# HGRN2 values in two passes over pairs of token tiles, with value-weight buffers of their own

## The chip, the cores and the metric

The kernel runs on one core of one Trainium2 chip. The metric is the device time of one execution in microseconds (us), lower is better. Times are medians of several executions; the trace comes from one further execution that was profiled. In the trace, PE is TensorE (PEld its weight loads), DVE is VectorE, ACT is ScalarE, POOL is GpSimd, SP is SyncE, which here issues the DMAs of the weights.

## The reference, cut to what matters

The reference is one layer of a hybrid decoder trunk on 512 tokens with a model width of 1024, all in float32:

```
h = rmsnorm(x)
z = h @ w_in                       # columns: q, f, i (values), g of HGRN2, then those of MLA and two gates
o_a = hgrn2(q, f, i, g)            # 8 heads, key and value width 128, recurrent state
o_b = mla(...)                     # 8 heads of latent attention
x = x + (sigmoid(ga) * (o_a @ w_branch_hgrn) + sigmoid(gb) * (o_b @ w_branch_mla)) @ w_out
x = x + moe(rmsnorm(x))            # 64 experts in 8 groups, two per token
out = rmsnorm(x)
```

In HGRN2 each head has a query, a decay (f), a value (i) and an output gate (g), each a projection of h with 1024 x 128 weights. The value of head h is `h @ w_in[:, 2048 + 128 h : 2048 + 128 (h + 1)]`, used as it is, with no nonlinearity.

## The kernel before, in words

The 512 tokens are T = 4 tiles of 128; the width of 1024 is KT = 8 tiles of 128. Most projections are made to near float32 precision from two rounded halves: a weight block comes by DMA into a raw buffer, ACT rounds it into a high part (`split`, L90) and another engine, here mostly POOL, takes the difference as the low part (L91). A product is then three matmuls: high by high, high by low, low by high. The normalised input lies transposed in SBUF in the same two parts (`hT`).

**The order of the stages.** Latent projections and rotary parts, latent attention (`mla`), HGRN2 (`hgrn`), the two branch products with their gates (L204 to L230), the output product with the routing (L249 to L273), and the mixture of experts (`moe`), in which the expert weights are streamed from HBM through a ring of buffers. No order is written out by hand around the change: the framework's scheduler gives each engine a fixed order at compile time, in which instructions that come earlier in the program go first where both are ready, and later ones fill the gaps. On the chip each engine works its own order off and waits at an instruction whose inputs are late.

**HGRN2.** For each head, `project` (L678) makes three projections by `proj` (L635): the decay, the query and the gate. Each loads 512 KB of weights with `wtile` (L275), splits them, and runs 24 matmuls of 512 columns into a PSUM tile `z`. The pool of `z` tiles (`zps`, L155) has two buffers. The pool of the weights (`wp`, L157) has two buffers each of `wraw`, `whi` and `wlo`, 4 KB per partition each; a raw buffer is free when POOL has taken the low part, a `whi`/`wlo` pair is free when its matmuls are done. All weight loads go through SP in order. The body of a head (L711 to L806) is a chain of small DVE products (L717, L719, L762, L763, L778, L791 among them), each followed by small matmuls into `lv` and `mx1`, copies by ACT (L771, L773, L784, L789), and at its end the norm of the head's output: squares on ACT (L801), `rsqrt` on DVE (L105, L114), a scaling on ACT (L805). `close` (L666) transposes that output and multiplies it by the gate, one head later.

**The values.** They are made for two heads at a time, 256 columns wide, by `value_weights` and `values`. The first call (L408, L449) is made ahead of the attention, for heads 0 and 1. The others are made in `hgrn` at L704, when h is 1, 3 and 5, ahead of the projections of head h + 1. In the scheduled order their matmuls fill the gaps of the body of head h - 1, so the bodies of heads 0, 2 and 4 have values beside them, and the projections of head h + 1 follow. `value_weights` makes two blocks of 512 rows by 256 columns with `wtile`, so it takes both `whi` and both `wlo` buffers. `values` takes both `z` tiles, of two token tiles each, and runs over the weight tiles outside and over all four token tiles inside, 96 matmuls of 256 columns; then ACT copies both `z` tiles to `vh` (L632).

Of the kernel before, what the change touches and what calls it, by code (L numbers as in the profile page):

```python
# [10 lines left out]
F32 = mybir.dt.float32  # L11
F32R = mybir.dt.float32r
# [8 lines left out]
T = S // 128  # L21
KT = D // 128
# [54 lines left out]
class Trunk:  # L77
# [206 lines left out]
    def latent(self, st, gl, hT, wp):  # L284

        tc, nc, a, ident, sm, gT = self.tc, self.nc, self.a, self.ident, self.sm, self.gT
        w_in = a["w_in"][0]
# [10 lines left out]
        with tc.tile_pool(name="c", bufs=1, reuse_waits="tile") as cp, tc.tile_pool(name="cps", bufs=4, space=PSUM, reuse_waits="tile") as cps:  # L298
# [40 lines left out]
            ps = cps.tile([128, 8], F32, name="tr", bufs=2)  # L339
# [37 lines left out]
            for t in range(T):  # L377
                if t + 1 < T:
                    columns_of(t + 1)
                ps = cps.tile([128, QR], F32, name="c")  # L380
# [10 lines left out]
            for t in range(T):  # L391
                ps = zps.tile([128, CW - QR], F32, name="z") if t < 2 else cps.tile([128, CW - QR], F32, name="c")
                project(ps, wk, t)
                cacc.append(ps)
            ps = cps.tile([128, 38], F32, name="tr", bufs=2)
# [12 lines left out]
            vw = self.value_weights(wp, 0)  # L408
# [37 lines left out]
                        nc.tensor.transpose(tr[:, h], qs[:, i * 4 + h].rearrange("p a c -> p (a c)"), self.identr)  # L446
                    nc.scalar.copy(out=qpT[:, i * 4:i * 4 + 4, t * 128:(t + 1) * 128], in_=tr)

            self.vals = {0: self.values(hT, vw, self.hv)}  # L449


            a0, a1 = gT[:, 8:16], gT[:, 16:24]
# [62 lines left out]
    def mla(self, lat, obT, wp, hT):  # L515
# [6 lines left out]
        with tc.tile_pool(name="att", bufs=2, reuse_waits="tile") as ap, \  # L522
# [19 lines left out]
            def heads(h):  # L542
# [14 lines left out]
                return qT, kT  # L557

            values_of = {0: values(0)}
            qk = heads(0)  # L560
            for h in range(H):
                qT, kT = qk
                if h % 2 == 1 and h + 1 < H:
                    values_of[h + 1] = values(h + 1)
# [42 lines left out]
            e.tensor_tensor(out=u, in0=y, in1=sin, op=OP.mult)  # L607
            e.tensor_tensor(out=o, in0=t, in1=u, op=op)

    def value_weights(self, wp, h):  # L610

        w_in = self.a["w_in"][0]
        return [self.wtile(wp, w_in[kp * 512:(kp + 1) * 512, 2048 + h * 128:2048 + h * 128 + 256], 4, 256,
                           self.nc.gpsimd) for kp in range(KT // 4)]

    def values(self, hT, weights, pool):

        nc = self.nc
        v = pool.tile([128, T, 256], F32, name="vh", bufs=1)
        ps = [self.zps.tile([128, 2, 256], F32, name="z") for _ in range(2)]  # L620
        for kp, (hi, lo) in enumerate(weights):
            for k in range(4):
                kt = kp * 4 + k
                for t in range(T):
                    ts = slice(t * 128, (t + 1) * 128)
                    L, R = [hT[0][:, kt, ts], hT[1][:, kt, ts]], [hi[:, k], lo[:, k]]
                    for n, (l, r) in enumerate(((0, 0), (0, 1), (1, 0))):
                        nc.tensor.matmul(ps[t // 2][:, t % 2], lhsT=L[l], rhs=R[r],
                                         start=(kt == 0 and n == 0 and t % 2 == 0),
                                         stop=(kt == KT - 1 and n == 2), skip_group_check=True)  # L630
        for u in range(2):
            nc.scalar.copy(out=v[:, 2 * u:2 * u + 2], in_=ps[u])  # L632
        return v

    def proj(self, hT, wp, c0):  # L635
# [18 lines left out]
    def hgrn(self, st, hT, oaT, wp):  # L654
        tc, nc, a, ident, sm = self.tc, self.nc, self.a, self.ident, self.sm
        gT, lb, oml = self.gT, self.lb, self.oml
        w_in = a["w_in"][0]
        hg = st.enter_context(tc.tile_pool(name="hg", bufs=1, reuse_waits="tile"))
# [37 lines left out]
        vals = self.vals  # L696
        self.open = None
        now = project(0)
        for h in range(H):
            P, k, qq, g = now  # L700
            q3 = qq[:, :, 0:128]
            vh = vals[h - h % 2]
            if h % 2 == 1 and h + 1 < H:
                vals[h + 1] = self.values(hT, self.value_weights(wp, h + 1), (self.hv, hg)[(h + 1) // 2 % 2])  # L704
            if h + 1 < H:
                now = project(h + 1)
            close()
# [25 lines left out]
            for m, c0 in ((2, 64), (8, 256)):  # L733
                ks = hg.tile([128, S], F32, name="ks", bufs=2)
# [14 lines left out]
                for d, l0, l1 in ((1, 0, 96), (2, 96, 160), (3, 160, 192)):  # L749
                    w = (4 - d) * m  # L750
# [7 lines left out]
            for m in (32, 64):  # L758
                nb = S // (2 * m)
                ks = hg.tile([128, nb, m], F32, name="ks", bufs=2)  # L760
# [5 lines left out]
                for b in range(nb):  # L766
                    r = (b * 2 * m) % 128
                    c = (0 if m == 32 else 128) + (b * 2 * m) // 128 * m
                    self.mm(x1[r:r + m, c:c + m], ks[:, b], qp[:, b], True, True)
            for r in (0, 64):  # L770
                nc.scalar.copy(out=at[r:r + 32, :, r + 32:r + 64],  # L771
                               in_=x1[r:r + 32, 0:128].rearrange("p (t j) -> p t j", t=T))
# [3 lines left out]
            ks = hg.tile([128, T - 1, 128], F32, name="ks", bufs=2)  # L776
# [513 lines left out]
```

## Time and profile before

| what | us |
|---|---|
| median of 3 runs | 1615.59 |
| lowest and highest of them | 1612.76, 1617.44 |
| the profiled execution, its own time | 1614.09 |
| span of the profiled execution, first to last instruction | 1612.3 |
| PE busy in the span | 1389.1 (86%) |
| DVE, ACT, POOL busy | 595.7, 342.7, 268.1 |

The profiled execution lies 1.79 us above its own span and 1.50 us below the median of the runs. A busy share over the whole span mixes stages with different limits, so the rows further down take the stages one by one. In a row of a timeline the columns are start, duration, engine, line, operation, output from input, shape and count, and in brackets the idle time before it with what ended that.

### The profile page before, as it was taken

The numbers are of one execution on the slowest core, as the hardware profiler recorded it, in microseconds if no ns is written. First come the engines' busy times: TensorE is split into PE (matmuls) and PEld (weight loads), VectorE is DVE, ScalarE is ACT, GpSimd is POOL, SyncE is SP. The second block draws the span as 40 slices with busy tenths as digits, with TensorE's granted clock in tenths as the row PEclk, the third lists the DMA queues.
The fourth block names the chain that finished last, engine by engine and source line by source line (L and its number), as shares of the span: only waits on it lengthen the run. The fifth ranks groups of instructions, "written<-read, shape, count | busy, mean of one in ns | idle before, by whom it ended". The sixth has DMA issues, their size and how long they took to land. (4 is left out here: it accounts for less than half of the span.)

```text
span 1612.3 us, 20371 instructions
## 1 busy us (share of the span) xinstructions
PE 1389.1 (86%) x8282; PEld 846.0 (52%) x8282; DVE 595.7 (37%) x1444; ACT 342.7 (21%) x754; POOL 268.1 (17%) x294
## 2 busy tenths in 40 slices
PE   5999999999999999988897798788688788779784
PEld 5878787778788889933333133133233223223322
DVE  7648686676873333531120120120211112012023
ACT  5456523332242322420000000010000000000012
POOL 4321233332100000021110111011011011011012
PEclk9999999999999999998998899898898899899897
DMA  6111232222144337599999999999999999999995
GB/s 185 58 44 34 57 85 66 66 66 66 53 134 136 97 92 270 230 398 430 430 428 429 430 428 428 429 429 430 429 428 429 429 429 428 429 428 428 430 418 189
DMA packets 124767, 456.35 MB, mean 283 GB/s; under 512 B 11854, under 2 KB 93436, under 8 KB 97532
## 3 DMA queue, kind: packets, MB, share of 16 engines
q1 hardware_dynamic: 121852, 454.52, 70.4%
q8 instruction: 67, 1.10, 0.3%
q10 hardware_dynamic: 2816, 0.47, 0.2%
q14 instruction: 32, 0.26, 0.0%
HBM read 452.87 MB, written 2.10 MB: 282 GB/s over the span
## 5 line engine op out<-in xcount | busy, mean ns | idle before, releaser
L82 PE MATMUL h<-ck,xT 128*32 128x512 f32 x2048 | 313.7, 667 | 122.0 <-DMA ck<-in_expert_w 107.4
L82 PEld LDWEIGHTS h<-ck,xT 128*32 128x32 f32 x2048 | 75.2, 121 | 347.2 <-issue 164.6
L1104 POOL TENSOR_SCALAR t<-cst,slb,wts 128x128 f32<-128x128 f32 x64 | 50.4, 791 | 964.4 <-PE ga L1085 709.4
L1165 DVE TENSOR_TENSOR x<-cb,x 128x512 f32<-128x512 f32 x120 | 82.9, 691 | 289.0 <-PE cb L82 289.0
L82 PE MATMUL y<-ck,hid 128*32 128x512 f32 (+2 forms) x1088 | 170.4, 584 | 16.0 <-ACT hid L1144 9.4
L91 POOL TENSOR_TENSOR wlo<-wraw,whi 128x1024 fp32r<-128x1024 f32 (+3 forms) x52 | 97.6, 1877 | 213.4 <-ACT whi L90 185.8
L82 PE MATMUL z<-hTh,whi 128*128 128x512 f32 x320 | 127.7, 399 | 5.4 <-ACT vh L632 5.3
L1085 PEld LDWEIGHTS ga<-t,wo 128*128 128x128 f32 x1024 | 117.1, 192 | 25.5 <-issue 24.1
L82 PE MATMUL z<-hTh,wlo 128*128 128x512 f32 x320 | 126.7, 396 | 0.0
L82 PE MATMUL z<-hTl,whi 128*128 128x512 f32 x320 | 126.2, 394 | 0.0
L1085 PE MATMUL ga<-t,wo 128*128 128x128 f32 x1024 | 123.2, 278 | 1.2 <-DVE t L1082 1.2
L82 PE MATMUL cb<-xT,owT 128*128 128x512 f32 (+2 forms) x256 | 120.9, 604 | 2.4 <-DVE xT L1181 2.2
L90 ACT CAST whi<-wraw 128x1024 fp32r<-128x1024 f32 (+3 forms) x84 | 77.5, 922 | 172.9 <-PE z L82 94.5
L1139 DVE TENSOR_TENSOR t<-h,t 128x512 f32<-128x512 f32 x16 | 11.1, 691 | 258.9 <-PE h L82 258.9
L82 PEld LDWEIGHTS y<-ck,hid 128*32 128x32 f32 x1088 | 43.8, 111 | 110.0 <-issue 92.3
L82 PEld LDWEIGHTS cb<-xT,owT 128*128 128x128 f32 x256 | 40.3, 188 | 83.5 <-DVE x L1165 46.9
L1161 ACT COPY xT<-y 128x512 f32<-128x512 f32 x30 | 17.6, 585 | 257.4 <-PE y L82 257.4
L1144 ACT COPY hid<-ga 128x512 f32<-128x512 f32 x16 | 9.4, 585 | 293.6 <-PE ga L1142 293.6
L82 PEld LDWEIGHTS z<-hTh,whi 128*128 128x128 f32 x320 | 60.7, 190 | 18.2 <-ACT vh L632 5.9
L1138 DVE TENSOR_TENSOR t<-h,t 128x512 f32<-128x512 f32 x16 | 11.1, 691 | 155.6 <-ACT t L1137 155.6
L82 PEld LDWEIGHTS z<-hTh,wlo 128*128 128x128 f32 x320 | 60.4, 189 | 12.4
L82 PEld LDWEIGHTS z<-hTl,whi 128*128 128x128 f32 x320 | 60.6, 189 | 11.7
(352 smaller groups left out, 2185.0 us busy)
## 6 DMA issues: line engine op xcount, KB each, us to landing
ck<-in_expert_w SPq DMA_DIRECT2D x164, 2048.0 KB, 34.0
ck<-in_expert_w SPq DMA_DIRECT2D x52, 1024.0 KB, 15.0
wraw<-in_w_in SPq DMA_DIRECT2D x48, 512.0 KB, 4.0
wraw<-in_w_branch_mla SPq DMA_DIRECT2D x8, 512.0 KB
wraw<-in_w_branch_hgrn SPq DMA_DIRECT2D x8, 512.0 KB, 4.0
wo<-in_w_out SPq DMA_DIRECT2D x8, 512.0 KB, 6.1
xt<-in_x SPq DMA_DIRECT2D x4, 512.0 KB, 7.5
wraw<-in_mla_w_ukv SPq DMA_DIRECT2D x16, 128.0 KB, 2.5
```

The source lines that it names most:

```text
L82: self.nc.tensor.matmul(ps, lhsT=l, rhs=r, start=start, stop=stop)
L90: self.nc.scalar.copy(out=hi, in_=src)
L91: (eng or self.nc.vector).tensor_sub(out=lo, in0=src, in1=hi)
L1085: nc.tensor.matmul(ps[kt // 4][:, kt % 4], lhsT=self.h2[t][:, kt], rhs=oh[:, t], start=(t == 0 and kt % 4 == 0), stop=(t == T - 1), skip_g ...
L1104: nc.gpsimd.tensor_scalar(out=ow[:, t], in0=iota, scalar1=slot(t, 0), scalar2=wts[:, t, 0:1], op0=OP.is_equal, op1=OP.mult)
L1138: nc.vector.tensor_mul(out=sg, in0=rows(h1), in1=sg)
L1139: nc.vector.tensor_mul(out=sg, in0=rows(h3), in1=sg)
L1144: nc.scalar.copy(out=hid, in_=ps)
L1161: nc.scalar.copy(out=ysb[:, hs], in_=y[half])
L1165: nc.vector.tensor_add(out=self.x2[:, t, hs], in0=ps, in1=self.x2[:, t, hs])
```

## The change

The values are computed for token tiles 0 and 1 over all eight weight tiles, copied out, and then for token tiles 2 and 3. Each pass takes one `z` tile. The first call, ahead of the attention, passes `(range(T),)` and stays one pass over all four tiles. For the three calls in `hgrn`, the high and low parts of the value weights get tiles of their own in the pool `hg`, `vwh` and `vwl` of 8 KB per partition each and one buffer each; the raw weights still come through `wraw` and SP, and ACT and POOL still split them in two blocks.

```diff
-            self.vals = {0: self.values(hT, vw, self.hv)}
+            self.vals = {0: self.values(hT, vw, self.hv, (range(T),))}
...
-    def value_weights(self, wp, h):
-
-        w_in = self.a["w_in"][0]
-        return [self.wtile(wp, w_in[kp * 512:(kp + 1) * 512, 2048 + h * 128:2048 + h * 128 + 256], 4, 256,
-                           self.nc.gpsimd) for kp in range(KT // 4)]
-
-    def values(self, hT, weights, pool):
+    def value_weights(self, wp, h, pool=None):
+
+        src = lambda kp: self.a["w_in"][0][kp * 512:(kp + 1) * 512, 2048 + h * 128:2048 + h * 128 + 256]
+        if pool is None:
+            return [self.wtile(wp, src(kp), 4, 256, self.nc.gpsimd) for kp in range(2)]
+        hi, lo = [pool.tile([128, KT, 256], F32R, name=f"vw{i}") for i in "hl"]
+        for kp in range(2):
+            raw = wp.tile([128, 4, 256], F32, name="wraw")
+            self.nc.sync.dma_start(out=raw, in_=src(kp).rearrange("(k p) c -> p k c", p=128))
+            ks = slice(kp * 4, kp * 4 + 4)
+            self.split(raw, hi[:, ks], lo[:, ks], self.nc.gpsimd)
+        return [(hi[:, kp * 4:kp * 4 + 4], lo[:, kp * 4:kp * 4 + 4]) for kp in range(2)]
+
+    def values(self, hT, weights, pool, pairs=((0, 1), (2, 3))):

         nc = self.nc
         v = pool.tile([128, T, 256], F32, name="vh", bufs=1)
-        ps = [self.zps.tile([128, 2, 256], F32, name="z") for _ in range(2)]
-        for kp, (hi, lo) in enumerate(weights):
-            for k in range(4):
-                kt = kp * 4 + k
-                for t in range(T):
+        for ts_ in pairs:
+            ps = [self.zps.tile([128, 2, 256], F32, name="z") for _ in ts_[::2]]
+            for kt in range(KT):
+                hi, lo = [w[:, kt % 4] for w in weights[kt // 4]]
+                for t in ts_:
                     ts = slice(t * 128, (t + 1) * 128)
-                    L, R = [hT[0][:, kt, ts], hT[1][:, kt, ts]], [hi[:, k], lo[:, k]]
-                    for n, (l, r) in enumerate(((0, 0), (0, 1), (1, 0))):
-                        nc.tensor.matmul(ps[t // 2][:, t % 2], lhsT=L[l], rhs=R[r],
+                    for n, (l, r) in enumerate(((0, hi), (0, lo), (1, hi))):
+                        nc.tensor.matmul(ps[t // 2 - ts_[0] // 2][:, t % 2], lhsT=hT[l][:, kt, ts], rhs=r,
                                          start=(kt == 0 and n == 0 and t % 2 == 0),
                                          stop=(kt == KT - 1 and n == 2), skip_group_check=True)
-        for u in range(2):
-            nc.scalar.copy(out=v[:, 2 * u:2 * u + 2], in_=ps[u])
+            for u, z in enumerate(ps, ts_[0] // 2):
+                nc.scalar.copy(out=v[:, 2 * u:2 * u + 2], in_=z)
         return v
...
-                vals[h + 1] = self.values(hT, self.value_weights(wp, h + 1), (self.hv, hg)[(h + 1) // 2 % 2])
+                vals[h + 1] = self.values(hT, self.value_weights(wp, h + 1, hg), (self.hv, hg)[(h + 1) // 2 % 2])
```

## Rows read from the trace of the kernel before

**Rows 1.** Busy time of each engine in four stretches: HGRN2, the branch products, the output product with the routing, and the experts. Columns: stretch, its length, busy time (and count) of PE, PEld, DVE, ACT, POOL, then the granted TensorE clock, the busy share of the DMA engines and GB/s.

```profile
180.00:465.00 285.00, 270.94 (x1616) 230.20 (x1615) 208.13 (x484) 93.04 (x229) 72.68 (x36) 0.99 0.23 62
465.00:612.00 147.00, 146.85 (x649) 120.98 (x648) 56.68 (x85) 44.16 (x75) 0.00 (x0) 1.00 0.41 122
612.00:700.00 88.00, 87.08 (x700) 78.55 (x702) 42.32 (x179) 31.31 (x58) 5.87 (x9) 1.00 0.74 282
700.00:1612.00 912.00, 732.48 (x4428) 282.84 (x4419) 164.91 (x378) 77.80 (x177) 132.32 (x192) 0.91 0.99 418
```

**Rows 2.** What PE waited for between 180 and 465 us: waiting line and what released it, us in total, times, the longest.

```profile
PE z L82 <- ACT vh L632: 5.3, 3, 1.8
PE mx L674 <- ACT on L805: 3.7, 3, 1.2
PE mx L82 <- DVE ks L762: 2.6, 6, 0.5
PE lv L82 <- DVE at L729: 2.1, 7, 0.4
```

**Rows 3.** Timeline of PE around the first and the third of the waits for `vh`: the last value matmul, the first projection matmul behind it, and matmuls of the same kind later.

```profile
245.33 0.28 PE L628 MATMUL z<-whi,hTl 128*128 128x256 f32 x1
247.37 0.50 PE L82 MATMUL z<-hTh,whi 128*128 128x512 f32 x1 [1.76 <-ACT vh L632]
...
382.65 0.50 PE L82 MATMUL z<-hTh,whi 128*128 128x512 f32 x1 [1.79 <-ACT vh L632]
...
384.04 0.63 PE L82 MATMUL z<-hTl,whi 128*128 128x512 f32 x1
384.47 0.63 PE L82 MATMUL z<-hTh,wlo 128*128 128x512 f32 x1
...
387.33 0.40 PE L82 MATMUL z<-hTl,whi 128*128 128x512 f32 x1
387.57 0.39 PE L82 MATMUL z<-hTh,wlo 128*128 128x512 f32 x1
```

**Rows 4.** Two stretches, one around the first wait and one behind the third; columns as in rows 1.

```profile
245.00:249.00 4.00, 2.24 (x13) 1.78 (x12) 1.84 (x7) 3.05 (x7) 0.17 (x1) 1.00 0.51 129
...
383.50:386.50 3.00, 3.00 (x8) 2.32 (x8) 0.00 (x0) 0.53 (x1) 2.36 (x1) 0.50 0.00 0
```

**Rows 5.** Timeline of ACT: the two casts of value weights, and the work between the norm of head 0 and the copies of the values.

```profile
219.42 1.05 ACT L90 CAST whi<-wraw 128x1024 fp32r<-128x1024 f32 x1 [4.30 <-PE z L82]
...
224.86 1.04 ACT L90 CAST whi<-wraw 128x1024 fp32r<-128x1024 f32 x1 [3.90 <-PE z L82]
...
245.70 1.14 ACT L805 ACTIVATE on<-mx,rs_y 128x128 f32<-128x128 f32 x4 [4.71 <-DVE rs_y L114]
246.71 1.09 ACT L632 COPY vh<-z 128x512 f32<-128x512 f32 x2
```

**Rows 6.** The DVE product L105 inside the norm: all of its instructions between 180 and 465 us (duration in ns, minimum, median, maximum), and the one of head 0.

```profile
L105 DVE TENSOR_TENSOR rs_u<-rs_u,oss x14: 141/180/2395, 241.5 to 448.7; 128x4 f32<-128x4 f32 x14
...
241.50 2.36 DVE L105 TENSOR_TENSOR rs_u<-rs_u,oss 128x4 f32<-128x4 f32 x1
```

**Rows 7.** Timeline of POOL: the low parts of the weights of the gate of head 1, of the two value blocks, and of the decay of head 2.

```profile
214.70 2.40 POOL L91 TENSOR_TENSOR wlo<-wraw,whi 128x1024 fp32r<-128x1024 f32 x1 [2.90 <-ACT whi L90]
220.55 2.39 POOL L91 TENSOR_TENSOR wlo<-wraw,whi 128x1024 fp32r<-128x1024 f32 x1 [3.44 <-ACT whi L90]
225.98 2.37 POOL L91 TENSOR_TENSOR wlo<-wraw,whi 128x1024 fp32r<-128x1024 f32 x1 [3.04 <-ACT whi L90]
241.07 2.78 POOL L91 TENSOR_TENSOR wlo<-wraw,whi 128x1024 fp32r<-128x1024 f32 x1 [6.67 <-ACT whi L90]
```

**Rows 8.** SP and the weight loads: what SP waited for between 180 and 465 us, two of its issues (the second value block for heads 2 and 3, the first for heads 4 and 5), and the loads of that stretch with their count, KB each and median us from issue to landing.

```profile
SPq L278 <- POOL wlo L91: 227.7, 28, 20.7
...
217.13 0.37 SPq L278 DMA_DIRECT2D wraw<-in_w_in  x1
...
267.83 0.37 SPq L278 DMA_DIRECT2D wraw<-in_w_in  x1
...
wraw<-in_w_in SPq DMA_DIRECT2D x30, 512.0 KB, 4.0
```

**Rows 9.** Products of the chain on DVE: all of L762 between 180 and 465 us (ns, minimum, median, maximum), then three instructions of head 0 and one of head 1.

```profile
L762 DVE TENSOR_TENSOR ks<-k,Sx x16: 415/425/987, 227.6 to 456.5; 128x256 f32<-128x256 f32 x16
...
227.65 0.98 DVE L762 TENSOR_TENSOR ks<-k,Sx 128x256 f32<-128x256 f32 x1
...
230.67 0.42 DVE L762 TENSOR_TENSOR ks<-k,Sx 128x256 f32<-128x256 f32 x1
...
231.23 0.45 DVE L763 TENSOR_TENSOR qp<-qq,f 128x256 f32<-128x256 f32 x1
...
273.05 0.55 DVE L778 TENSOR_TENSOR ks<-k,Sx 128x384 f32<-128x384 f32 x1
```

**Rows 10.** The matmuls on PE that use those products: three groups of head 0 and one of head 1.

```profile
228.69 0.44 PE L82 MATMUL mx<-qp,ks 128*32 128x32 f32 x16 [0.48 <-DVE ks L762]
229.42 1.54 PE L82 MATMUL lv<-gq,ks 128*128 128x192 f32 x8 [0.29 <-DVE at L729]
...
232.07 0.68 PE L82 MATMUL mx<-qp,ks 128*64 128x64 f32 x8
...
274.44 0.49 PE L782 MATMUL mx<-cst,ks 128*128 128x128 f32 x3
```

## The prediction

> **What bounds the kernel now.** I read the stretches first. The reader is to see that the bound changes hands once: up to 700 us PE is busy nearly all the time (270.94 of 285 us in HGRN2, 146.85 of 147, 87.08 of 88), and from 700 us on the DMA engines are busy for 0.99 of the time at 418 GB/s [rows 1]. The change touches only HGRN2, so what PE gains or loses there moves the start of the expert stream, whose bytes stay the same, and with it the end, one for one. Next I read what PE waited for in HGRN2: 5.3 + 3.7 + 2.6 + 2.1 = 13.7 us [rows 2], nearly all of the 285 - 270.94 = 14.1 us of idle time. The largest item is the one that the change aims at: three times, the first projection behind the values waits 1.8 us for the copy `vh`. The timelines show why. The values hold both `z` tiles to their last matmul at 245.33; ACT, which works in order, does the scaling `on` at 245.70 and only then, at 246.71, the copies [rows 3, 5]. `on` was itself late, since the norm's L105 took 2.36 us where its fastest takes 0.14 [rows 6]: it sat beside the POOL split at 241.07, which ended at 243.85, and L105 ended at 243.86 [rows 7]. So a DVE product of two SBUF operands can stand still for the rest of a POOL split. That is the second thing that the reader should keep.
>
> **The change, part by part.** It removes no matmul, cast, split or DMA, and adds none; it moves them.
>
> The wait for `vh`. The first pass ends about half-way through the 96 value matmuls, and its copy runs while the second pass covers it. The projection behind needs that first `z` tile, so the wait goes: 3 x 1.77 = 5.3 us [rows 2]. Next in line behind it would be the projection's weights, split by 243.85 already now [rows 7], ahead of 245.6 where the values end; with the change earlier still. The second copy may keep its place behind `on`; its tile is needed only by the query projection, a whole projection later (24 matmuls at 0.24 us, 5.8 us) [rows 3]. If that cover were gone, the cost would be the same 1.8.
>
> The clock. Behind the third wait the matmuls of the projection follow each other at 0.43 us instead of 0.24 [rows 3]; the granted clock is 0.50 there, the lower level of 1.2 GHz, where behind the first it stays at 1.00 [rows 4]. Eight matmuls at that pace cost 8 x 0.19 = 1.5 us. In this execution that goes with the wait: 1.5 us, with 0 as the other end, as only one of three equal waits had it.
>
> The splits. Today the value blocks are cast when a `whi` buffer comes free, at 219.42 and 224.86 [rows 5], and the low parts follow on POOL [rows 7]. With buffers of their own they go as soon as the raw block is there; then the decay and the query of the next head can take the `whi` buffers that came free at those times. The raw buffers are the limit now: SP waits 227.7 us for low parts in all, and a load takes 4.0 us to land [rows 8]. For head 2: the second value block, issued at 217.13, lands at 221.1, is cast in 1.05 us and split in 2.4, to 224.6. That frees its raw buffer for the query's weights: landed at 228.6, cast by 229.7, split on POOL from 229.7 to 232.1. The decay's split fits between, 224.7 to 227.1. The same happens for heads 4 and 6.
>
> What this gives: the split that now runs at 225.98 makes the first L762 take 0.98 us instead of 0.43 [rows 7, 9], and PE loses 0.48 + 0.29 there [rows 10]. With POOL free from 227.1 to 229.7, that goes: 3 x 0.77 = 2.3 us.
>
> What it takes: the query's split now lies in the chain of head 0. The second L762, 0.55 us earlier than today at 230.1, would stand until 232.1; L763 ends 1.0 us behind its start as today [rows 9], at 233.1. PE would come to the matmuls that need it 0.77 us earlier than 232.07 [rows 10], at 231.3: a wait of 1.8 us, three times, 5.4 us. PE's order is fixed, so value matmuls placed later can't fill it.
>
> For heads 4 to 7 the first value block moves too: issued at 267.83 [rows 8], landed at 271.8, cast by 272.9, split until 275.3, beside the chain of head 1. L778, now 273.05 to 273.60, would end at 275.85; PE needs it at 274.44 [rows 9, 10], so 1.4 us, for heads 1 and 3: 2.8 us. For heads 2 and 3 that block lands while only projections run; nothing is lost.
>
> No row shows a split at these places, so each of the five waits is bounded by 0 (POOL done before the chain or past it) and by 2.4, a whole split [rows 7]; the nearest row is L762, where 0.55 us of standing became 0.48 of PE wait [rows 9, 10], so I take the worked values. By the Trainium skill (SBUF — State Buffer, Who interferes with whom) a VectorE instruction with two SBUF inputs is held off until a GpSimd instruction that started first is through; L105 agrees. By that rule alone, with no slack on PE, the five would cost 5 x 2.4 = 12.0 us and the sum would be a loss of 2.9 us.
>
> At nothing I cost the 16 KB per partition more in `hg` (its space was that of the attention, over by then), the first call (same order) and the three waits for `on` at L674, in heads without values.
>
> **The sum:** 5.3 + 1.5 + 2.3 - 5.4 - 2.8 = 0.9 us less. Against the profiled execution, 1614.09, that is 1613.2; it lies 1.5 below the median of 1615.59, so the median after should be **1614.7**. With both ends of the unknowns (five waits from 0 to 12.0, clock 0 to 1.5): 9.1 us less to 4.4 more, 1606.5 to 1620.0.
>
> **Rivals.** *The splits miss the chain.* A transfer that lands sooner or a scheduled order that puts the casts elsewhere would leave the gains alone: 5.3 + 2.3 + 1.5 = 9.1, 1606.5; with half of the five waits (4.1), 1610.6. For it: ACT is idle most of HGRN2 (93 of 285 us busy) and the chain has gaps. Against: eight heads show no slack at L762, and the raw loads leave little freedom.
>
> *The splits cost more than the waits, and the clock falls behind them* (slower). Each of the five stalls is the whole 2.4 us, and one in three is followed by the lower clock at 1.5 us, as today: 12.0 + 5/3 x 1.5 = 14.5, less 9.1, is 5.4 more: 1621.0. It decides against the change by more than the bound below once stall and clock together average (9.1 + 4.8) / 5 = 2.8 us. Against it: PE waits of 1.2 us [rows 2] are in a stretch whose mean clock is 0.99 [rows 1]. The Trainium skill (TensorE: Matmul & The Clock Gate, What's actually happening) ties the rate to how busy the engine has lately been; by it stalls amid value matmuls could cost clock. The trace has one fall in three and no more.
>
> *The copy does not move.* If the schedule puts the first copy behind `on` all the same, the 5.3 us and the 1.5 stay: with the splits as above 8.2 - 2.3 = 5.9 more, 1621.5, without them 1613.3. ACT waits 4.71 us ahead of `on` with nothing to do [rows 5], time enough for the copy, so I give it little.
>
> **How the numbers follow.** A measurement of this kernel tells about 0.3% (4.8 us) from no change. Forecast, half or more given back: 0.50. Splits miss the chain: 0.30. Slower: 0.14. Copy not moved: 0.06. Faster by over 0.3% (below 1610.8) is most of the first rival and the lower edge of the forecast, 0.29 + 0.07 = 0.36; slower (above 1620.4) is the slower rival and half of the last, 0.14 + 0.03 = 0.17; the rest, 0.47, is no change. The range takes in the first rival and most of the forecast's upper bound: 1606.5 to 1620.0, the forecast's own being 1611 to 1618.
>
> **What would show it.** Right: no PE wait for `vh` at all; the second pass of value matmuls running while ACT copies the first; two POOL splits, for decay and query, ahead of or in the body of heads 0, 2 and 4, where now there is one; a DVE product of the chain (L717, L762 or L778) of over 1 us inside the second, and a PE wait behind it; one more such in heads 1 and 3; the expert stream starting about 1 us earlier. Wrong: PE idle in HGRN2 down by 5 us or more (first rival), or new waits of over 14 us in sum (slower rival), or a `vh` wait that stays.

## The result, and the profile after

| | before | after |
|---|---|---|
| median, us (6 runs each) | 1614.40 | 1623.67 |
| lowest to highest | 1611.32 to 1617.44 | 1621.66 to 1625.31 |
| the profiled execution, and its span | 1614.09, 1612.3 | 1623.53, 1621.7 |

The change makes the kernel slower: the ratio is 1.0053, with a 95% interval of 1.0040 to 1.0066. The forecast was 1614.7 with a range up to 1620.0, so the result lies above the range. One execution of this study, the profiled one of e7 below, took 3411.04 us and is left out of every figure. What follows compares the two profiled executions, 9.4 us apart. Line numbers from L628 on are larger by 6 after the change (the wait for L762 of before is one for L768 of after).

The first and the third of the stretches of [rows 1]:

```profile
180.00:465.00 285.00, 265.86 (x1567) 225.79 (x1566) 208.57 (x474) 89.06 (x215) 72.07 (x36) 0.98 0.21 61
...
612.00:700.00 88.00, 87.23 (x667) 82.34 (x669) 43.14 (x178) 32.95 (x60) 0.00 (x0) 1.00 0.70 268
```

PE is idle for 5.1 us more in HGRN2 (265.86 busy against 270.94), at a lower mean clock. The second row shows that the experts start later: POOL, which had 5.87 us of expert work before 700 us, has none there now. The waits of PE between 180 and 465 us, as in [rows 2]:

```profile
PE mx L680 <- ACT on L811: 7.1, 3, 2.9
PE mx L82 <- DVE ks L768: 6.2, 6, 4.1
PE mx L788 <- DVE ks L784: 2.1, 2, 1.1
...
PE z L82 <- POOL wlo L91: 1.5, 1, 1.5
```

The row for `vh` (5.3 us) is gone. In its place stand a single wait of 4.1 us for `ks`, two of 2.9 for `on`, two of 1.1 for `ks` of L784, and one for a low part. PE's timeline shows both sides of this: the projection now follows the last value matmul of the second pass without a gap (compare [rows 3]), and of the new waits one of 4.09 lies in head 0, those of 2.91 in heads 1 and 3.

```profile
232.60 0.64 PE L82 MATMUL mx<-qp,ks 128*32 128x32 f32 x16 [4.09 <-DVE ks L768]
...
251.91 0.28 PE L634 MATMUL z<-vwh,hTl 128*128 128x256 f32 x1
252.03 0.39 PE L82 MATMUL z<-hTh,whi 128*128 128x512 f32 x1
...
293.49 1.24 PE L680 MATMUL mx<-cst,on 128*128 128x128 f32 x4 [2.91 <-ACT on L811]
...
363.32 1.10 PE L680 MATMUL mx<-cst,on 128*128 128x128 f32 x4 [2.91 <-ACT on L811]
```

**Head 0: the wait of 4.09.** ACT works in order. Its timeline after the change, and the one row of before that answers to the last (`g<-z` is the sigmoid of the gate, L692 before, L698 after):

```profile
221.10 1.05 ACT L90 CAST vwh<-wraw 128x1024 fp32r<-128x1024 f32 x1 [4.71 <-DMA wraw<-in_w_in]
223.95 1.06 ACT L90 CAST whi<-wraw 128x1024 fp32r<-128x1024 f32 x1 [1.30 <-DMA wraw<-in_w_in]
228.80 1.04 ACT L90 CAST whi<-wraw 128x1024 fp32r<-128x1024 f32 x1 [3.79 <-DMA wraw<-in_w_in]
229.75 0.59 ACT L698 ACTIVATE g<-z 128x512 f32<-128x512 f32 x1
```

```profile
225.81 0.59 ACT L692 ACTIVATE g<-z 128x512 f32<-128x512 f32 x1
```

All three casts now wait for a DMA; before, the cast ahead of this sigmoid waited for PE to free a `whi` [rows 5]. The third is that of the query's weights for head 2, and ACT stands at it for 3.79 us, with the sigmoid of the gate of head 1 behind it, which before was through 3.9 us earlier. The load is late because its raw buffer was still being read by the split of the second value block:

```profile
222.23 2.41 POOL L91 TENSOR_TENSOR vwl<-wraw,vwh 128x1024 fp32r<-128x1024 f32 x1 [2.27 <-ACT vwh L90]
...
224.66 3.17 SPq L278 DMA_DIRECT2D wraw<-in_w_in  x2
...
229.92 2.35 POOL L91 TENSOR_TENSOR wlo<-wraw,whi 128x1024 fp32r<-128x1024 f32 x1 [2.48 <-ACT whi L90]
```

The split ends at 224.64, SP issues at 224.66, the block is there at 228.8. On DVE the product with the sigmoid stands ahead of the chain of head 0, whose first L768 comes at 231.58 instead of 227.65 [rows 9]:

```profile
230.37 0.69 DVE L699 TENSOR_TENSOR g<-z,g 128x512 f32<-128x512 f32 x1 [5.45 <-ACT g L698]
```

In heads 2 and 4 no such wait came. Their values' weights had been cast a head earlier, the query's load was in time, and the cast waited for PE to free its `whi`, as before (head 2: 4.88 us, to 301.20). Its split (302.33) lies beside the first L768, where the second value split lay before, and the waits there are the same 0.47 and 0.29.

**Heads 1 and 3.** POOL's splits there (rows of head 1), and the DVE products beside them:

```profile
277.06 2.65 POOL L91 TENSOR_TENSOR vwl<-wraw,vwh 128x1024 fp32r<-128x1024 f32 x1 [4.73 <-ACT vwh L90]
...
284.49 2.40 POOL L91 TENSOR_TENSOR vwl<-wraw,vwh 128x1024 fp32r<-128x1024 f32 x1 [3.78 <-ACT vwh L90]
286.95 2.49 POOL L91 TENSOR_TENSOR wlo<-wraw,whi 128x1024 fp32r<-128x1024 f32 x1
```

```profile
277.58 2.55 DVE L784 TENSOR_TENSOR ks<-k,Sx 128x384 f32<-128x384 f32 x1
...
284.65 2.53 DVE L723 TENSOR_TENSOR Sx<-Sx,f 128x256 f32<-128x256 f32 x1
287.11 2.35 DVE L808 TENSOR_SCALAR oss<-oss 128x4 f32<-128x4 f32 x1
```

The first split holds L784 (0.55 us before [rows 9]) and gives the wait of 1.06. The other two, the second value block's and that of the gate's weights for head 3, follow each other without a gap and hold two DVE instructions in turn. L808 is the first step of the norm, so PE waits 2.91 us for `on` instead of 1.24.

**The gate's low part.** In head 1's projections the first value block comes ahead of the gate's weights on ACT (the cast below, which waits for its load; the gate's follows at 215.35) and on POOL, where the gate's split follows the value block's without a gap. PE waits 1.53 us for it, to 220.01:

```profile
213.91 1.05 ACT L90 CAST vwh<-wraw 128x1024 fp32r<-128x1024 f32 x1 [5.77 <-DMA wraw<-in_w_in]
...
217.41 2.54 POOL L91 TENSOR_TENSOR wlo<-wraw,whi 128x1024 fp32r<-128x1024 f32 x1
```

**The clock.** Behind the wait of 4.09 and behind the first of 2.91, but not behind the second, PE runs at the lower level, 1.2 GHz (columns as in [rows 1]):

```profile
233.20:238.60 5.40, 5.31 (x23) 5.07 (x22) 4.72 (x14) 0.00 (x0) 0.04 (x1) 0.50 0.34 97
...
294.00:297.00 3.00, 3.00 (x9) 2.44 (x9) 2.93 (x6) 2.26 (x4) 1.78 (x1) 0.50 0.00 0
```

The low stretches reach somewhat further than these windows, to 239.0 and 297.1. Half of 5.4 + 3.0 us, 4.2 us, is an estimate of the loss. The delays against before bear it out: beyond what the waits account for, they grow by 2.9 us from 232.60 to L788 of head 0 (241.14), and by 1.3 us from 293.49 to the first `ks` matmuls of head 2 (305.03).

**The account.** New in HGRN2: 1.5 (gate's low part) + 3.3 (4.09 less the 0.48 + 0.29 of [rows 10]) + 2.1 (L784 twice) + 3.3 (`on`, twice 2.91 - 1.24) + 4.2 (clock) = 14.4. Gone: 5.3 (`vh`) + 1.5 (clock behind its third wait) = 6.8. The difference, 7.6, stands against 7.0 measured: the first closing transpose of the last head (L674, now L680) starts at 473.27 instead of 467.77, while this execution had entered HGRN2 1.5 us earlier (an ACT cast that comes at 202.70 before comes at 201.15). The rest of the 9.4 lies behind HGRN2: some 1.7 us before the routing, in which two new waits of 0.6 and 0.2 us stand, and 2.4 us in the stretch of the experts, whose length, from the first matmul into `h` to the last, varies from 880.3 to 883.3 us among the kernels here without pattern.

### The profile page after: what moved, and what is told of

It reads as the page before. It is cut to its first block, busy times and chain, and to the rows that moved or that the text cites. A ratio compares the mean times of both kernels' runs of the same rounds, so it can differ in the third digit from the quotient of the medians.

```text
span 1621.7 us, 20363 instructions
## 1 busy us (share of the span) xinstructions
PE 1391.6 (86%) x8282; PEld 848.2 (52%) x8282; DVE 598.5 (37%) x1444; ACT 343.0 (21%) x754; POOL 267.6 (16%) x294
## 5 line engine op out<-in xcount | busy, mean ns | idle before, releaser
L91 POOL TENSOR_TENSOR wlo<-wraw,whi 128x1024 fp32r<-128x1024 f32 (+3 forms) x46 | 82.2, 1787 | 206.8 <-ACT whi L90 185.2
L90 ACT CAST whi<-wraw 128x1024 fp32r<-128x1024 f32 (+3 forms) x78 | 71.0, 910 | 165.7 <-PE z L82 76.4
```

Source lines behind the costliest of these rows:

```text
L90: self.nc.scalar.copy(out=hi, in_=src)
L91: (eng or self.nc.vector).tensor_sub(out=lo, in0=src, in1=hi)
```

## The experiments

Four theories stood against each other. **A**: buffers of their own let casts, splits and loads run ahead, and the engines, each working its queue off in order, then hold up the chain. **B**: the order in two passes itself costs something. **C**: the two new tiles move others in memory, and that costs. **D**: the old wait for `vh` came from the order of ACT, not from the single pass. All ratios are to the kernel before, run in the same five rounds on the same chip; the medians of before lay between 1615.47 and 1615.87.

| kernel | median, us | ratio, 95% interval |
|---|---|---|
| e1_two_pass_shared | 1610.65 | 0.9971, 0.9960 to 0.9983 |
| e2_own_one_pass | 1627.14 | 1.0080, 1.0065 to 1.0095 |
| e3_proj_casts_late | 1616.78 | 1.0009, 0.9996 to 1.0021 |
| e4_value_splits_late | 1620.93 | 1.0034, 1.0021 to 1.0046 |
| e5_both_late | 1608.83 | 0.9962, 0.9947 to 0.9976 |
| e6_vals_late_4to7 | 1625.27 | 1.0063, 1.0050 to 1.0076 |
| e7_before_pad | 1616.75 | 1.0003, 0.9991 to 1.0015 |
| e8_before_vh_dve | 1615.81 | 0.9999, 0.9990 to 1.0008 |
| e9_own_raw | 1610.96 | 0.9974, 0.9961 to 0.9986 |
| e10_late_own_raw | 1613.61 | 0.9986, 0.9976 to 0.9996 |
| e12_own_raw_first_late | 1610.17 | 0.9969, 0.9958 to 0.9980 |

### One half of the change at a time: e1 and e2

e1 is the kernel after, with the two passes but the weights through the shared `whi` and `wlo`:

```diff
-  self.values(hT, self.value_weights(wp, h + 1, hg), ...)
+  self.values(hT, self.value_weights(wp, h + 1), ...)
```

> The two passes alone: values for token tiles 0-1, then 2-3, but the split value weights stay in the shared whi/wlo buffers. Theory A (the loss comes from the own buffers, which let casts and splits of value, decay and query weights run ahead of work that is needed sooner): the ACT order stays nearly that of before, the vh waits (5.3 us) go, and a new wait of at most about 1 us behind each values block comes, since the decay's weights can be split only when the first value block is free at three quarters of the values. Result 1 to 6 us below before, no PE wait over 1.5 us in heads 0 to 5 but those of before. Theory B (the order of the two passes itself costs, for example 48 matmuls in a row into one PSUM tile): as slow as after, 8 to 10 us above before.

It is faster than before by 0.0029, 4.7 us. Its waits between 180 and 465 us:

```profile
PE mx L680 <- ACT on L811: 3.7, 3, 1.2
PE mx L82 <- DVE ks L768: 2.6, 6, 0.5
...
PE z L82 <- POOL wlo L91: 1.4, 3, 0.5
```

These are the waits of [rows 2] without the one for `vh`, and 1.4 us more for low parts, each at most 0.5. So the two passes do what they should, and B falls: the loss is in the buffers.

e2 is the other half, own buffers and one pass over all four tiles:

```diff
-  ..., (self.hv, hg)[(h + 1) // 2 % 2])
+  ..., (self.hv, hg)[(h + 1) // 2 % 2], (range(T),))
```

> The own buffers alone, values in one pass over four tiles as before. Theory A: all new waits of after stay (about 4.1 us at the first ks product of head 0, 1.0 at the transposes and 2.9 before the closing transposes of heads 1 and 3, 1.5 for a low part in the gate projection of head 1), and the copies vh come back as a wait where the scaling of the norm is ahead of them: 9 to 16 us above before. Theory B: with the old order the time is that of before within 2 us.

It has the highest ratio of all (its interval overlaps that of e6), and has the new waits of after, the one for `ks` longer still; but the wait for `vh` that was expected to come back did not. Waits first, then PE's timeline where the values of heads 2 and 3 end:

```profile
PE mx L680 <- ACT on L811: 7.3, 3, 3.0
PE mx L82 <- DVE ks L768: 7.2, 6, 5.1
```

```profile
251.75 0.28 PE L634 MATMUL z<-vwh,hTl 128*128 128x256 f32 x1
251.99 0.50 PE L82 MATMUL z<-hTh,whi 128*128 128x512 f32 x1
```

The projection follows after a quarter of a microsecond, with one pass as with two: ACT began `on` at 249.91 and was through at 251.06, ahead of the last value matmul, so it stood ready for the copies. That speaks for D: where `on` is not late, a single pass makes no wait.

### Which queue: e3, e4, e5 and e6

e3 is after, but the three projections of heads 2, 4 and 6 are issued (loads, casts and splits included) only behind the squares of the norm of the head whose body is running:

```diff
+            if h % 2 == 1 and h + 1 < H:
+                with tc.issue_after(squared[h - 1]):
+                    now = project(h + 1)
-            if h + 1 < H:
+            elif h + 1 < H:
                 now = project(h + 1)
```

> After, with the ACT work of the projections behind the values (heads 2, 4, 6) held behind the squares of the norm of the head before, so that their casts no longer stand ahead of the gate's sigmoid waiting for a load. Theory A: the 4.1 us wait of head 0 falls to 0.8 or less and the low clock behind it goes; the waits of heads 1 and 3 (1.0 and 2.9) and the 1.5 us for the low part stay. 5 to 8 us below after, so 1 to 4 above before. If instead the 4.1 us come from POOL holding DVE off, the wait stays at 3 us or more and the time is that of after.

The ratio falls by 0.0044, 7.1 us. The wait of 4.1 is gone, and `ks` of L772 (L768 of after) costs 1.2 us in three waits; what is left are the waits of heads 1 and 3 (7.3 and 2.2 in their rows), the gate's low part (1.7), and the clock, which here falls to 0.50 behind both waits of 3 us for `on`:

```profile
PE mx L680 <- ACT on L815: 7.3, 3, 3.0
...
PE mx L82 <- DVE ks L772: 1.2, 3, 0.4
```

e3 takes the query's split out of head 0's chain together with its cast, so it does not by itself tell ACT's order from POOL holding DVE; e9 below does.

e4 holds back the value casts and splits alone: behind the gate's split of head 1 for heads 2 and 3, and behind the scaling `on` of head h - 2 for the others.

```diff
+                if h == 1:
+                    with tc.issue_after(self.g_split[0]), tc.issue_after(self.g_split[1]):
+                        vw = self.value_weights(wp, h + 1, hg)
+                else:
+                    with tc.issue_after(scaled[h - 2]):
+                        vw = self.value_weights(wp, h + 1, hg)
```

> After, with only the value weights' casts and splits held back: behind the split of the gate's weights for heads 2 and 3, behind the scaling of the norm two heads back for heads 4 to 7. Theory A: the 1.5 us wait of PE for a low part and the extra 1.0 and 1.7 us in heads 1 and 3 go (5.5 to 7 us with the low clock), the 4.1 us wait in head 0 stays; the casts for heads 4 and 6 come later and could put a POOL split into the chain of heads 2 and 4 (up to 1.5 us each). 2 to 7 us below after, 2 to 7 above before.

The waits of heads 1 and 3 and the one for the gate's low part are gone, as they should be, but the one in head 0 stays (4.51), and heads 2 and 4 have two new ones of 2.7:

```profile
PE lv L82 <- DVE at L744: 6.7, 6, 2.7
PE mx L82 <- DVE ks L777: 5.9, 5, 4.5
```

What happens in head 2 is what happens in head 0. ACT, in its rows here, stands at a cast of the projections, and behind it is the gate's sigmoid (L700 in this kernel):

```profile
298.83 1.05 ACT L90 CAST whi<-wraw 128x1024 fp32r<-128x1024 f32 x1 [4.64 <-DMA wraw<-in_w_in]
299.79 0.59 ACT L700 ACTIVATE g<-z 128x512 f32<-128x512 f32 x1
```

So neither hold alone is enough: whichever cast stands first in ACT's queue with its load not there holds the rest.

e5 does both:

> After, with both moves undone on ACT and POOL: the projections' casts behind the squares of the norm as in e3, and the value weights' casts behind the split of the gate's weights (heads 2 and 3) or behind the scaling of the norm two heads back (heads 4 to 7). Theory A: all new waits go and the gain of 5.3 us (and of 1.5 of low clock) stays: 4 to 8 us below before. Theory B (two passes cost in themselves, or the moved tiles): above before.

It has the lowest ratio of the study, 6.1 us under before; its interval overlaps those of e1, e9 and e12, so it can't be called faster than these. Its waits:

```profile
PE mx L681 <- ACT on L823: 3.9, 4, 1.2
PE lv L82 <- DVE at L747: 3.2, 7, 0.9
PE mx L82 <- DVE ks L780: 1.2, 3, 0.4
```

No wait is above 1.25 us, and the mean clock of 180 to 465 us is 1.00. So A accounts for the loss: with the order held, the change gains about what it took out of [rows 2].

e6 holds the value casts back only for heads 4 to 7 (the second branch of e4's edit):

> As e4, but only for the values of heads 4 to 7. Theory A: as e4, but the 1.5 us wait for a low part of the gate's weights stays: 1 to 2 us above e4.

It came out 4.3 us above e4 where 1 to 2 were expected. The gate's low part costs 1.9 us again, as expected, and the waits for `ks` (5.8 in six) and `at` (6.9 in seven) come to the same as in e4. The two profiled executions are 2.0 us apart, about this wait; what the rest of the 4.3 is was not found.

### The load behind the cast: e9, e10 and e12

If ACT stood at the query's cast because its raw buffer was taken, a raw buffer for the values alone should let it go. e9 is after with this line changed (4 KB per partition more):

```diff
-            raw = wp.tile([128, 4, 256], F32, name="wraw")
+            raw = pool.tile([128, 4, 256], F32, name="vwr", bufs=1)
```

> After, with the raw value weights in one buffer of their own in hg (4 KB per partition more), so that the loads of the decay's and the query's weights no longer wait for the value splits. Theory A (the 4.1 us wait of head 0 is ACT standing at the cast of the query's weights, ahead of the gate's sigmoid, until a load that waited for a value split has landed): the wait falls to about 1 us with nothing held back in ACT's order; the value splits, with a buffer of their own, also run earlier, among the projections, so that the waits of heads 1 and 3 go if they fall there: 2 to 8 us below before. If it was not the load, 3 us or more stay in head 0 and the time is within 4 us of after.

```profile
PE mx L680 <- ACT on L811: 3.7, 3, 1.2
PE mx L82 <- DVE ks L768: 2.9, 6, 0.8
PE z L82 <- DVE g L699: 2.3, 1, 2.3
```

The wait of 4.09 is down to 0.75, and those of heads 1 and 3 are back at 1.24. In ACT's rows the query's cast waits no longer for a DMA, but for its `whi` to come free from PE:

```profile
230.28 1.05 ACT L90 CAST whi<-wraw 128x1024 fp32r<-128x1024 f32 x1 [4.17 <-PE z L82]
```

A new wait of 2.28 came at 217.34: the first value block is now cast and split earlier, two POOL splits hold two DVE products of the chain (2.47 us at 209.69 and 2.50 at 212.19), and the gate's product L699, which frees the `z` tile, stands behind them (the expectation of e12 below puts it down to ACT's cast; the row that ends the wait is DVE's). The query's split, at 231.40, still lies beside the first L768 of head 0 (0.99 us), and the wait is 0.75: so the 4.09 did not come from POOL holding that product. The link from split to raw buffer to load to cast to sigmoid is shown, and the kernel with this one line changed is faster than before, though its schedule also has the value casts earlier.

e12 is e9 with the value casts for heads 2 and 3 behind the gate's split:

> e9, with the casts of the value weights for heads 2 and 3 alone held behind the split of the gate's weights of head 1, since in e9 the second of them stands on ACT ahead of the casts and sigmoids of head 1 until its load has landed (PE waits 2.3 us at 217 us). Theory A: that wait goes, up to 1 us may come back at the first chain of head 0: 1 to 3 us below e9, 5 to 9 below before.

The 2.28 went and a wait of 1.60 came in head 0. Its ratio can't be told from e9's. e10 is e5 with the raw buffer of its own:

> e5 (casts held back on ACT) with the raw buffer of its own as in e9. Theory A: about as e5, 4 to 8 us below before; the 0.85 us waits of heads 2 and 4 may go, as the value splits move.

It lost 0.0024 against e5, 3.9 us, where none was expected: in heads 2 and 4 PE waits 2.33 and 2.40 us for `at`, where e5 has 0.85. ACT's rows show why:

```profile
290.72 1.04 ACT L90 CAST vwh<-vwr 128x1024 fp32r<-128x1024 f32 x1 [5.04 <-DMA vwr<-in_w_in]
291.68 0.59 ACT L700 ACTIVATE g<-z 128x512 f32<-128x512 f32 x1
```

The new raw buffer is a single one, so the load of the second value block waits for the split of the first, its cast for the load, and the gate's sigmoid for the cast. A buffer that takes a wait away in one order makes one in another.

### The other theories: e7 and e8

e7 is the kernel before, with an unused tile of 16 KB per partition in `hg`, so that the tiles lie as far apart as after:

```diff
+            if h == 1:
+                pad = hg.tile([128, 2 * KT * 256], F32, name="pad")
+                nc.gpsimd.memset(pad[:, 0:8], 0.0)
```

> Before, with 16 KB per partition in the pool hg that nothing uses (one write of 8 elements), so that the tiles behind it lie where the change puts them. Theory A: no wait of HGRN2 changes; within 2 us of before, at most a little in the branch products behind it. Theory C (the moved tiles make later tiles wait for their release): 3 us or more above before, with waits behind 470 us.

No difference from before is seen, and by the interval none above 0.0015, that is 2.4 us. C falls as the cause of 9 us; e5, which has the new tiles in place and is faster than before, says the same. The waits of this kernel, whose profiled execution is the one left out, can't be compared, so that part of the expectation stays open.

e8 is the kernel before, with the later copies of `vh` on DVE:

```diff
-            nc.scalar.copy(out=v[:, 2 * u:2 * u + 2], in_=ps[u])
+            (nc.scalar.copy if pool is self.hv and not hasattr(self, 'vals') else nc.vector.tensor_copy)(...)
```

> Before, with the copies vh of the three later value calls on DVE instead of ACT. Theory D (the 1.8 us wait for vh is mostly ACT's order: the copies queue behind the scaling of the norm, which is late because a POOL split holds L105 off; the copy itself is the smaller part): the wait falls to 0.6 to 1.0 us, 2 to 4 us below before. If the wait is the copy and its latency, it stays at 1.5 or more and the time is that of before.

```profile
PE mx L674 <- ACT on L805: 5.4, 6, 1.2
...
PE z L82 <- DVE vh L632: 2.6, 3, 0.9
```

The three waits for `vh` fall from 1.77 to 0.86 us: half of each goes with ACT's order, as D says. The time did not move: three new waits of 0.55 us for `on` took 1.7 of the 2.7 us that came free, and the 1.0 left is less than the interval can show. The clock falls here too behind the third of them, to 0.50 from 382 to 385 us, though that wait is only 0.86. So D's mechanism is there, and alone it gains nothing that can be measured.

## Why the prediction was wrong

**Right.** The bound: what PE loses in HGRN2 moves the expert stream and the end, within some 2 us. The wait for `vh` went whole (5.3), and the lower clock behind its third case too. In head 0 the splits lie where they were worked out to lie: the second value block split until 224.6 (224.64 measured), the query's from 229.7 (229.92). So does head 1's first value split, until 275.3 (279.7, with the chain some 4 us later too). L784 stood under it for 2.55 us; 1.4 us of wait was priced, 1.06 and 1.03 measured.

**The steps that failed** are three terms that the working put at nothing. The forecast had HGRN2 0.9 us shorter, the account has it 7.6 longer. Of these 8.5 us, 4.2 are the clock, 3.3 the waits for `on` and 1.5 the gate's low part; the query's cast came out 0.2 dearer than priced, L784 0.7 cheaper.

The waits for `on` were put at nothing since those heads have no values. But they have the splits of the value weights, and these were followed on POOL only as far as the first. The second value split and the one of the gate's weights follow without a gap in heads 1 and 3 and reach the first step of the norm: 3.3 us. By the Trainium skill (SBUF — State Buffer, Who interferes with whom) VectorE's two-input products and, in some cases, its tensor_scalar are held while GpSimd has the shared ports; the trace agrees in both kinds, with L723 at 2.53 us where it takes 0.42 alone, and L808 at 2.35 where its median is 0.17.

For the value block of heads 2 and 3 the working said that it lands while only projections run and that nothing is lost. But the gate's cast and low part of head 1 then stand behind that block's on ACT and POOL (215.04 to 217.46, then 217.41 to 219.95): 1.5 us.

The clock was priced at 0 for the new waits in the forecast, and 5/3 x 1.5 us in the slower rival. It cost 4.2, behind two of the new waits and not behind the others. The slower rival, 1621.0 at a chance of 0.14, thus had the right sign and the right pair of causes (waits in the chain, then the clock), but its waits were five splits of 2.4 where the runs show one wait of 4.1, two of 2.9, two of 1.1 and one of 1.5.

**Right in size by luck.** The query's split in the chain of heads 0, 2 and 4 was priced as POOL holding the second L762, 3 x 1.8 = 5.4, with 3 x 0.77 = 2.3 to the good: 3.1 us in all, and 3.3 were measured. The rows show neither term. In heads 2 and 4 the waits of 0.48 and 0.29 stay as they were and none is added. In head 0 the second L768 did not stand (0.41 us, at 234.59); the cost is the wait of 4.09 us at the first, by another path. The prediction followed the cast of the query's weights (load, 228.6, 229.7) and costed what came after it on POOL, but not what stood after it on ACT. Behind a cast that waits for a load, ACT does nothing, and the next instruction was the sigmoid on which DVE and then the chain hang. e9 takes away the reason for the late load, with the query's cast still straight ahead of the sigmoid (4.09 to 0.75); e3 moves the cast behind the norm (no wait above 0.4 in that group). e4 and e10 then made the same wait elsewhere, at other casts. The gain was also set too high: in e5, with no split beside the first products of head 0, 0.22 of the 0.29 stays.

**Read too simply.** The wait for `vh` was put down to the single pass holding both `z` tiles. e8 shows that half of it goes with ACT's order, and in e2, where `on` is not late, none of it is left with the same single pass: ACT was held at `on`, which was late by the POOL split beside L105. The rows for that stood in the prediction; that a change of the casts' order would move this wait by itself was not drawn from them. Nor do all eight heads lack slack at L762, as the first rival has it: [rows 2] has six such waits, of at most 0.5 us.

**Open.** Why the clock falls behind the first wait of 2.91 us and not behind the second, and in e8 behind one of 0.86; the 1.7 us behind HGRN2 and the 2.4 us in the experts; the 4.3 us between e6 and e4. An e5 with the weights in the shared buffers was not run.

## What to carry to other kernels

Buffers of its own take away more than a wait: they take away what held a stage's loads, casts and splits back, and these then stand earlier in every in-order queue that they use. Before giving a stage its own buffers, list for each engine what will stand behind the moved instruction, and ask of each cast whether its load will be there; where it will not, tie the cast to a later instruction (e5) or give the raw data a buffer too (e9). Where the gain sought comes from the order of the products alone, take that alone first: e1 (0.9971) can't be told from e5 (0.9962), so no run here shows that the buffers gain anything beyond the two passes.

## What the runs showed of the hardware

A DVE TENSOR_SCALAR of 128x4 with one input, 0.17 us alone, took 2.35 us beside a POOL split; so small steps of a norm are held as two-input products are. Two splits without a gap held two DVE instructions in a row, 2.53 and 2.35 us; only the first of them was done between the splits.

The granted clock of TensorE, in an engine that is busy otherwise, fell to 0.50 behind some waits. After the change it was at 0.50 for over 5 us behind a wait of 4.09 us, and for 3 us behind one of two equal waits of 2.91 us. It fell behind both waits of 3 us for `on` in e3, behind one of three waits of 0.86 us in e8, and behind none in e12 (the longest 1.60 us) and e5 (1.25 us). The length of a wait alone did not decide it.
